# Ragged self-attention on one core: the prologue ahead of the loops is reordered

## The chip, the cores and the metric

The kernel runs on one core of a Trainium2 chip. The core has engines that run beside each other, each with an instruction queue of its own: TensorE (PE in the profile, with PEld for its weight loads), VectorE (DVE), ScalarE (ACT), GpSimd (POOL) and SyncE (SP), which here only issues DMAs and computes addresses. A "q" behind an engine's name (DVEq) means what its queue does itself: register loads, arithmetic on registers, semaphores, branches, issuing of DMAs. The metric is the time of one execution on the device in microseconds (us), a median over runs.

## The reference

32 sequences of up to 512 rows and 512 columns, each with a length drawn between 64 and 511. For each: project to queries, keys and values, then attention with 8 heads of 64 columns over the rows that are alive; rows past the length are zero in the output.

```python
for b in range(batch):
    seq_len = lengths[b]
    qkv = np.matmul(x[b, :seq_len], w_qkv)
    q, k, v = np.split(qkv, 3, axis=-1)          # each to (n_heads, seq_len, head_dim)
    scores = scale * np.matmul(q, k.transpose(0, 2, 1))
    attn = np.exp(scores - np.max(scores, axis=-1, keepdims=True))
    attn = attn / (np.sum(attn, axis=-1, keepdims=True) + 1e-08)
    output[b, :seq_len] = np.matmul(attn, v).transpose(1, 0, 2).reshape(seq_len, dim)
```

## The kernel before

The sequences are sorted by length on the chip, longest first, and worked off in pairs. There are loops for twelve lengths (512, 448, then 384 down to 96 in steps of 32); each handles the pairs whose longer sequence fits, so its trip count depends on the lengths and is read into registers of each engine at run time. A loop's body works on one sequence at a time (a "position", j = 0 or 1): scores `S` on PE, exponentials on ACT, `A` for attention times values; between them PE projects the next sequence: `Q`, `K` (line 228, `project`) and `V` (line 239, `values`). The order in a body is a string in `ORDER`.

The change touches only `before_loops`, the prologue (below: the head), and one line of setup. The head is a list of named operations, each with an engine, the resources it reads and writes, and code; the order of the list is the order on each engine's queue, and `plan_waits` works out from the resources which semaphores are to be waited on. So moving an operation in the list moves it on its own engine's queue only, and the waits follow.

What the head does, in the order of the data:

- Lengths come in (`row`, `col`); DVE ranks them (`key_row`, `least`, `rank`, `hit_i`, `hit_l`), PE spreads the sorted numbers over the partitions (line 446), DVE stores `order` and `slen`. `least` gives the longest sequence's number early, so that SP can fetch its four tiles of 128 rows (`x0.0` to `x0.3`, line 520).
- Weights in float32 come by DMA in halves (`wv`, `wq`, `wk`, line 336) and are cast to float16 in four chunks of 128 rows (`shorten`, line 622) on ACT and POOL. Every Q block needs all four chunks of W_q, every K block all four of W_k.
- Each tile of x0 is masked and cast (`cast_tile`, lines 280 to 285), transposed by four matmuls into a bank (`turn`, line 645) and copied out as `xT` (line 654). V0 to V3 need one tile each; Q0 to Q3 and K0 to K3 need all four. Their results go from a bank to SBUF by a copy (line 677).
- The second sequence, x1, is cast and transposed the same way (banks 3 to 6); the third, x2, is cast by POOL and transposed by DMA.
- From the sorted lengths DVE makes `more`, `counts`, `shifted`, `ends_f` and `ends`: the trip counts, packed in three words. `read_ends` (lines 594 to 616) loads each word into a register of an engine and takes it apart with shifts and masks.
- POOL fills the columns of `et` that a loop's exponentials leave out (14 memsets, line 479), and PE runs 24 matmuls on the identity (line 551) while nothing else is ready.

SP issues, in this order: lengths, W_v, x0's tiles, W_q, W_k, x1, x2. Banks are eight parts of PSUM; an operation that writes a bank waits for the copy that last read it. Before, K0 takes bank 1, which Q2 used.

Of the kernel before, what the change touches and what calls it, by code (L numbers as in the profile page):

```python
# [14 lines left out]
ALU = mybir.AluOpType  # L15
AX = mybir.AxisListType

P = 128
# [130 lines left out]
def kernel(  # L149
# [8 lines left out]
    nc = tc.nc  # L158
    B, MAXS, D = x.shape
# [38 lines left out]

    why = "sorted on the chip from indices 0 to 31, and counts of 0 to 16"

    WARM = 24
    LOOPS = [512, 448, *range(384, 64, -32)]

    ORDER = {
# [56 lines left out]
    def copy_on(act):  # L261
        return nc.scalar.copy if act else nc.vector.tensor_copy
# [33 lines left out]
    def before_loops():  # L296
# [4 lines left out]
        def op(name, eng, emit, reads=(), writes=(), dma=False):  # L301
            ops.append(Op(name, eng, emit, tuple(reads), tuple(writes), dma))

        def small(name, eng, emit, reads=(), shape=(B, B), dtype=FP32):

            t = const.tile(list(shape), dtype, name=f"h_{name}")
            op(name, eng, lambda: emit(t), reads, (name,))
            return t
# [20 lines left out]
            dma=True,  # L329
        )  # L330

        def weights(name, tile_, m0, c0, c1):
            op(
                f"{name}{c0}",
                "SP",
                lambda: sp.dma_start(out=tile_[:, c0:c1, :], in_=w_in[:, c0:c1, m0 : m0 + D]),
                (),
                [f"{name}.{c}" for c in range(c0, c1)],
                dma=True,
            )  # L340
# [5 lines left out]
        def iota(pattern, up, base=0):  # L346
# [35 lines left out]
        def copied(name, eng, source, after, shape=(B, B), dtype=FP32):  # L382
            return small(
                name, eng, lambda t: copy_on(eng == "ACT")(out=t, in_=source), after, shape, dtype
            )

        idx_f = copied("idx_f", "DVE", idx_i, ("idx_i",))
        idc_f = copied("idc_f", "DVE", idc_i, ("idc_i",), (B, 1))
        iota_f = copied("iota_f", "DVE", iota_i, ("iota_i",), (P, NT))
        ident16 = copied("ident16", "DVE", ident, ("ident",), (P, P), F16)  # L390

# [78 lines left out]
                :, :, N // 2 :  # L470
            ]

        for n in range(NT, 0, -1):
            N = min(N for N in LOOPS if tiles(N) == n)
            for e, et in enumerate(e_bufs if n > 1 else e_bufs[0:2]):
                op(
                    f"et{e}.{N}",
                    "POOL",
                    lambda et=et, N=N: pool.memset(left_out(et, N), 0x3C003C00),
                    ("order", f"et{e}"),  # L480
                    (f"et{e}",),
                )

        def mask(b, pos):
            op(
# [63 lines left out]
        def warm():  # L549
            for k in range(WARM):  # L550
                nc.tensor.matmul(banks[3][:, 0:P], ident16, ident16, start=True, stop=True)

        op("warm", "PE", warm, ("ident16",), ("bk3",))

        more = small(
            "more",
            "DVE",
            lambda t: dve.tensor_tensor(
                out=t,
                in0=slen.rearrange("p (j two) -> p j two", two=2)[:, :, 0]  # L560
                .unsqueeze(1)
                .broadcast_to([P, COUNTS, B // 2]),
                in1=limits,
                op=ALU.is_gt,
            ),
            ("slen", "limits"),
            (P, COUNTS, B // 2),
        )
        counts = small(
            "counts",  # L570
            "DVE",
            lambda t: dve.tensor_reduce(out=t, in_=more, axis=AX.X, op=ALU.add),
            ("more",),
            (P, COUNTS),
        )
        shifted = small(
            "shifted",
            "DVE",
            lambda t: dve.tensor_tensor(out=t, in0=counts, in1=shifts, op=ALU.mult),
            ("counts", "shifts"),  # L580
            (P, COUNTS),
        )
        ends_f = small(
            "ends_f",
            "DVE",
            lambda t: dve.tensor_reduce(
                out=t, in_=shifted.rearrange("p (g k) -> p g k", k=4), axis=AX.X, op=ALU.add
            ),
            ("shifted",),
            (P, COUNTS // 4),  # L590
        )
        op("ends", "DVE", lambda: dve.tensor_copy(out=ends_i, in_=ends_f), ("ends_f",), ("ends",))

        def read_ends(e, part=None):
            def load():
                eng = EN[e]
# [61 lines left out]
                (f"xT{b}.{t}",),  # L658
            )

        def step(name, bank, eng):
# [15 lines left out]
            op(name, eng, lambda: copy_on(eng == "ACT")(out=to, in_=of_), (bank,), (made,))  # L677
# [19 lines left out]
        def twos(source):  # L697
# [16 lines left out]
        op(  # L714
            "alive",
            "DVE",
# [19 lines left out]
            (P, B // 2),  # L736
        )
        joined("table", four, computed, 20, ("four", "computed"), table)
        step("V2", "bk4", "DVE")
        shorten("wq", w_q, 0, 2, "ACT")  # L740
        op(
            "M",
            "DVE",
# [35 lines left out]
        step("Q3", "bk6", "ACT")  # L779
        read_ends("PE", 1)  # L780
        read_ends("PE", 2)
# [11 lines left out]
        read_ends("SP")  # L793


        def casts():
# [15 lines left out]
        fetch("LD1", 0, 1, 3, 0, NT)  # L812


        op("joinPE", "PE", lambda: None, [f"xT1.{t}" for t in range(NT)], [f"bk{k}" for k in range(3, 7)])
# [6 lines left out]
    def tiles(N):  # L822
        return -(-N // P)
# [440 lines left out]
    with tc.tile_critical():  # L1264
# [100 lines left out]
```

## Time and profile before

| | |
|---|---|
| runs | 344.72, 345.69, 346.73 us; median 345.69 |
| profiled execution | 345.26 us, span 343.4 us |
| PE busy | 326.6 us, 95% |
| ACT, DVE, POOL busy | 262.7, 215.3, 97.9 us |
| first score matmul of the first loop | 22.73 us |
| DMA | 73.07 MB, mean 213 GB/s |

A timeline row reads: start and length in us, engine and line, operation, what it writes and reads, the shape, the count of merged instructions, and in brackets the idle time before it and what ended that. Line numbers are those of the kernel before. Matmuls overlap in these rows, so the stage's pace is the distance between starts. The trace begins a little after the execution does and ends before it: the profiled execution's 345.26 us hold 1.9 us that lie outside the span.

### The profile page before, as it was taken

To read this page: it belongs to the slowest core of one execution; us is meant where nothing else is said; L and a number is where in the kernel's file an instruction comes from. 1 tells how busy PE (TensorE), PEld (TensorE's weight loads), DVE (VectorE), ACT (ScalarE), POOL (GpSimd) and SP (SyncE) were. 2 spreads that over 40 slices of the span, in tenths; PEclk is the share of its full clock that TensorE was granted. 3 is DMA by queue.
4 is the path that set the end of the run, shared out by engine and by line. 5 is a ranking of instruction groups with operands and counts; after the bars stand their busy time and mean duration, and the time that the engine had idled before them with its cause. 6 is when DMAs were issued, how large, how long until landed. Compare 5 with 4: busy or idle time off the path is not lost.

```text
span 343.4 us, 10664 instructions
## 1 busy us (share of the span) xinstructions
PE 326.6 (95%) x3846; PEld 201.4 (59%) x3846; DVE 215.3 (63%) x657; ACT 262.7 (77%) x410; POOL 97.9 (29%) x124
## 2 busy tenths in 40 slices
PE   4999999999999999999999999999999999999971
PEld 3444545464555555556655656675677776777751
DVE  6556666667667565465555566677775547777664
ACT  4369899797877878889888898777567788678741
POOL 5466040404030330331133033113222342242311
PEclk9999999999999999999999999999999999999996
DMA  6975974483638936957849549869986656669742
GB/s 224 369 239 131 334 170 135 146 282 90 223 67 287 304 83 226 283 177 285 271 139 307 195 152 338 248 241 238 266 244 198 171 168 216 207 171 238 229 142 79
DMA packets 76060, 73.07 MB, mean 213 GB/s; under 512 B 45808, under 2 KB 45808, under 8 KB 76016
## 3 DMA queue, kind: packets, MB, share of 16 engines
q1 hardware_dynamic: 75968, 72.51, 72.4%
q8 instruction: 24, 0.39, 0.5%
q14 instruction: 20, 0.16, 0.2%
q10 hardware_dynamic: 48, 0.00, 0.0%
HBM read 28.32 MB, written 33.55 MB: 180 GB/s over the span
## 4 chain that ended last, share of the span: by engine, by line
PE 89%; DVE 3%; DMA 2%; issue 1%; SPq 1%; ACT 1%; DVEq 1%; POOL 0%; POOLq 0%
PE banks L228 36%; PE banks L239 21%; PE banks L1065 17%; PE banks L981 15%; DMA out_dram<-out_nat 1%; DVE out_nat L1086 1%; DMA x_nat<-in_x_dram 1%; SPq L255 1%; DVE rcp L1078 1%; DVE qz L677 1%; PE banks L645 1%; DVE v_aug L1039 0%; DVEq L600 0%; DVE rcp L1075 0%; DVE v_aug L677 0%
## 5 line engine op out<-in xcount | busy, mean ns | idle before, releaser
L995 ACT ACTIVATE et<-banks 128x704 f16<-128x704 f32 (+6 forms) x264 | 195.9, 813 | 37.6 <-PE banks L981 36.5
L285 POOL TENSOR_TENSOR x<-x_nat,mask 128x512 f16<-128x512 f32 x87 | 88.3, 1039 | 233.6 <-DVE mask L874 218.3
L228 PE MATMUL banks<-xT,w_r 128*128 128x352 f16 (+11 forms) x1024 | 146.5, 288 | 1.5 <-ACT qz L1023 0.6
L228 PEld LDWEIGHTS banks<-xT,w_r 128*128 128x128 f16 x1024 | 85.0, 98 | 41.6 <-issue 8.7
L239 PE MATMUL banks<-w_r,xT 128*128 128x512 f16 x332 | 85.2, 382 | 0.4 <-ACT xT L654 0.2
L1065 PEld LDWEIGHTS banks<-v_aug,et 128*128 128x128 f16 x1792 | 66.2, 98 | 22.6 <-issue 7.7
L1065 PE MATMUL banks<-v_aug,et 128*128 128x65 f16 x1792 | 74.3, 194 | 1.0 <-ACT et L995 0.7
L1086 DVE TENSOR_TENSOR out_nat<-banks,rcp 128x256 f32<-128x256 f32 (+1 forms) x136 | 64.1, 472 | 5.9 <-DMA out_dram<-out_nat 1.3
L981 PE MATMUL banks<-qz,kT 64*128 64x352 f16 (+11 forms) x640 | 61.6, 298 | 2.8 <-DVE out_nat L1086 1.8
L1075 DVE RECIPROCAL rcp<-banks 128x4 f32<-128x4 f32 (+1 forms) x136 | 25.1, 185 | 44.4 <-PE banks L1065 43.2
L1039 DVE CAST v_aug<-banks 128x512 f16<-128x512 f32 x58 | 40.1, 692 | 18.4 <-PE banks L239 18.2
L239 PEld LDWEIGHTS banks<-w_r,xT 128*128 128x128 f16 x332 | 28.3, 98 | 30.9 <-issue 4.6
L981 PEld LDWEIGHTS banks<-qz,kT 64*128 64x128 f16 x640 | 23.1, 94 | 34.0 <-issue 26.0
L1023 DVE CAST qz<-banks 128x352 f16<-128x352 f32 (+4 forms) x39 | 22.8, 586 | 27.4 <-PE banks L228 27.4
L1023 ACT CAST kT<-banks 128x352 f16<-128x352 f32 (+4 forms) x55 | 26.8, 488 | 13.7 <-PE banks L228 12.8
L1078 DVE TENSOR_TENSOR rcp<-rcp,v_aug 128x4 f32<-128x4 f32 (+1 forms) x136 | 26.1, 192 | 4.7
L1023 ACT CAST qz<-banks 128x320 f16<-128x320 f32 (+5 forms) x52 | 24.5, 477 | 4.9 <-PE banks L228 3.6
L1023 DVE CAST kT<-banks 128x320 f16<-128x320 f32 (+4 forms) x36 | 19.9, 556 | 8.2 <-PE banks L228 7.3
L1039 ACT CAST v_aug<-banks 128x512 f16<-128x512 f32 x21 | 12.5, 596 | 6.1 <-PE banks L239 5.8
L874 DVE TENSOR_SCALAR mask<-alive 128x4 f32 x32 | 5.9, 184 | 5.9 <-issue 5.9
L950 DVE TENSOR_SCALAR v_aug<-alive 128x24 f16 (+3 forms) x32 | 7.2, 224 | 0.0
L446 PE MATMUL banks<-h_hit_i,h_ones 32*128 32x32 f16 x1 | 0.2, 203 | 4.7 <-DVE h_hit_i L429 4.7
(68 smaller groups left out, 48.9 us busy)
## 6 DMA issues: line engine op xcount, KB each, us to landing
x_nat<-in_x_dram SPq DMA_DIRECT2D x12, 768.0 KB, 5.6
out_dram<-out_nat SPq DMA_DIRECT2D x12, 768.0 KB, 4.0
x_nat<-in_x_dram SPq DMA_DIRECT2D x14, 512.0 KB, 4.0
x_nat<-in_x_dram SPq DMA_DIRECT2D x7, 1024.0 KB, 6.7
out_dram<-zeros SPq DMA_DIRECT2D x12, 512.0 KB, 5.4
out_dram<-out_nat SPq DMA_DIRECT2D x12, 512.0 KB, 3.0
out_dram<-out_nat SPq DMA_DIRECT2D x4, 1024.0 KB, 4.7
out_dram<-zeros SPq DMA_DIRECT2D x12, 256.0 KB, 5.4
```

What stands on the lines that cost most here:

```text
L228: last = nc.tensor.matmul(dst[:, 0:N], w_r[:, c, w0 : w0 + P], xT[:, c, 0:N], start=(c == 0), stop=(c == NC - 1),)
L239: last = nc.tensor.matmul(pv, xT[:, c, t * P : (t + 1) * P], w_r[:, c, 2 * D : 3 * D], start=(c == 0), stop=(c == NC - 1),)
L285: return engine.tensor_tensor(out=x16, in0=x32, in1=live.broadcast_to([P, D]), op=ALU.mult)
L950: return nc.vector.tensor_scalar(out=v_bufs[o][:, 0:n, :, HD], in0=alive[:, bass.ds(at("DVE") + (j + 1), 1), 0:n] .rearrange("p o t -> p ( ...
L981: last = nc.tensor.matmul(psc[par][:, x * n128 : x * n128 + N], kT[r, i, kt * P : (kt + 1) * P], qz[r, i, 0:N], start=True, stop=True,)
L995: return nc.scalar.activation(out=et[:, :, x0:x1, 0:N], in_=got.rearrange("p j (x q) -> p j x q", q=n128)[:, :, x0:x1, 0:N], func=AF.Exp, ...
L1023: return copy_on(act)(out=buf[:, ms, 0:N], in_=bank[:, 0 : gm * N].rearrange("p (m q) -> p m q", q=N),)
L1039: return copy_on(act)(out=v_bufs[o][:, t, :, 0:HD], in_=bank.rearrange("p (h d) -> p h d", d=HD))
L1065: last = nc.tensor.matmul(pav[:, g, qt, :], e_bufs[e][:, c0 + qt * P : c0 + (qt + 1) * P], v_aug[:, kt, h, :], start=(kt == 0), stop=(kt = ...
L1075: return nc.vector.reciprocal(out=rcp, in_=pav[:, :, :, HD])
L1078: return nc.vector.tensor_tensor(out=rcp, in0=rcp, in1=v_aug[:, 0:n, h0 : h0 + heads, HD].rearrange("p t g -> p g t"), op=ALU.mult,)
L1086: return nc.vector.tensor_tensor(out=o_t[:, 0:n, h0 * HD : (h0 + heads) * HD].rearrange("p t (g d) -> p g t d", d=HD), in0=pav[:, :, :, 0:HD],
```

## The change

All of it lies ahead of the loops:

- W_q is fetched by two DMAs from ACT's queue, behind ACT's cast of W_v's chunk 0; on SP, W_k's follow x0's directly. W_v's chunks 1 and 3 are cast by POOL instead of ACT.
- PE's 24 matmuls on the identity become four groups: 6 on `ones` over 512 columns as soon as that is set, 7 on the identity over 512 columns, and 5 and 6 over 128 columns between the first transposes and V0.
- POOL's 14 fills come in three parts: 4 after `ends`, 5 after W_q's casts, 5 after W_k's.
- `shifted`, `ends_f` and `ends` move on DVE from before x0's first cast to behind its third.
- Each engine reads its three words of loop ends at different places between its other work (DVE, ACT and POOL had read all three at once).
- x0's last tile is cast by DVE instead of POOL; V1 and V2 stand on PE before that tile's transposes, and the copies of V0 and V1 are moved behind other work on DVE.
- K0 to K3 use banks 3, 4, 5 and 7. x1's transposes stand between K1 and K2 (before: between K2 and K3), in the order 0, 1, 3, 2, through banks 0, 1, 2 and 6. x1's casts go to DVE, ACT, POOL, DVE (before: POOL, DVE, POOL, ACT). Q1's copy goes to ACT; K3's to DVE.
- `idc_f` is cast by ACT, followed by 16 increments of an otherwise unused semaphore on its queue; the semaphore increments that set up DVE's counts are made by SP.

```diff
-    WARM = 24
+        def spaced(e, count):
+            def pad():
+                for _ in range(count):
+                    EN[e].sem_inc(passed, 1)
+            op(f"spaced{e}{len(ops)}", e, pad)
...
+        def warm(name, source, count, repeats, after):
+            rows = source.shape[0]
+            wide = source.unsqueeze(1).broadcast_to([rows, repeats, P])
+            out = banks[3][:, 0 : repeats * P].rearrange("p (r q) -> p r q", q=P)
+            def matmuls():
+                for k in range(count):
+                    last = nc.tensor.matmul(out, source, wide, start=True, stop=True)
+                return last
+            op(name, "PE", matmuls, after, ("bk3",))
+        warm("warm0", ones16, 6, 4, ("ones",))
...
-        idc_f = copied("idc_f", "DVE", idc_i, ("idc_i",), (B, 1))
+        idc_f = copied("idc_f", "ACT", idc_i, ("idc_i",), (B, 1))
+        spaced("ACT", 16)
...
-        weights("wq", w_q, 0, 0, NC // 2)
-        weights("wq", w_q, 0, NC // 2, NC)
         weights("wk", w_k, D, 0, NC // 2)
         weights("wk", w_k, D, NC // 2, NC)
...
+        warm("warm1", ident16, 7, 4, ("ident16",))
...
-        for c in range(NC):
-            shorten("wv", w_v, 2 * D, c, "ACT")
+        shorten("wv", w_v, 2 * D, 0, "ACT")
+        shorten("wv", w_v, 2 * D, 1, "POOL")
+        weights("wq", w_q, 0, 0, NC // 2, "ACT")
+        weights("wq", w_q, 0, NC // 2, NC, "ACT")
+        shorten("wv", w_v, 2 * D, 2, "ACT")
+        shorten("wv", w_v, 2 * D, 3, "POOL")
+        (more, counts)
         cast_tile(0, 0, "DVE")
...
         turn(0, 0, "bk4", "DVE")
+        warm("warm2", ident16, 5, 1, ("ident16",))
         turn(0, 1, "bk5", "ACT")
+        warm("warm3", ident16, 6, 1, ("ident16",))
         cast_tile(0, 2, "DVE")
-        cast_tile(0, 3, "POOL")
-        step("V0", "bk0", "DVE")
+        (shifted, ends_f, ends)
+        copy_V0 = step("V0", "bk0", "DVE", True)
         turn(0, 2, "bk6", "DVE")
+        cast_tile(0, 3, "DVE")
+        copy_V0()
+        read_ends("ACT", 0)
+        read_ends("ACT", 1)
+        fill(4, ("ends",))
+        copy_V1 = step("V1", "bk1", "DVE", True)
+        copy_V2 = step("V2", "bk4", "DVE", True)
+        turn(0, 3, "bk3", "DVE")
+        copy_V1()
         shorten("wq", w_q, 0, 0, "ACT")
-        step("V1", "bk1", "DVE")
-        turn(0, 3, "bk3", "ACT")
         shorten("wq", w_q, 0, 1, "POOL")
+        read_ends("POOL", 0)
+        shorten("wq", w_q, 0, 2, "ACT")
+        shorten("wq", w_q, 0, 3, "POOL")
+        read_ends("POOL", 1)
+        fill(5, ())
+        step("V3", "bk5", "ACT")
+        copy_V2()
+        read_ends("ACT", 2)
+        read_ends("DVE", 0)
...
-        read_ends("DVE")
-        step("V3", "bk5", "ACT")
-        read_ends("ACT")
-        shorten("wq", w_q, 0, 3, "POOL")
         shorten("wk", w_k, D, 0, "POOL")
-        shorten("wk", w_k, D, 2, "POOL")
+        shorten("wk", w_k, D, 1, "POOL")
         step("Q0", "bk2", "DVE")
         fetch("x2", 0, 1, 1, 0, NT)
-        shorten("wk", w_k, D, 1, "POOL")
-        step("Q1", "bk0", "DVE")
+        read_ends("DVE", 1)
+        step("Q1", "bk0", "ACT")
         read_ends("PE", 0)
+        shorten("wk", w_k, D, 2, "POOL")
         shorten("wk", w_k, D, 3, "ACT")
+        fill(5, ())
         step("Q2", "bk1", "DVE")
-        read_ends("POOL")
-        cast_tile(1, 0, "POOL")
-        cast_tile(1, 2, "POOL")
+        read_ends("PE", 1)
+        read_ends("POOL", 2)
         step("Q3", "bk6", "ACT")
-        read_ends("PE", 1)
         read_ends("PE", 2)
-        cast_tile(1, 1, "DVE")
-        step("K0", "bk1", "DVE")
-        cast_tile(1, 3, "ACT")
-        step("K1", "bk2", "ACT")
-        step("K2", "bk0", "DVE")
-        for t, (bank, eng) in enumerate(
-            (("bk3", "DVE"), ("bk4", "ACT"), ("bk5", "DVE"), ("bk6", "ACT"))
-        ):
+        cast_tile(1, 0, "DVE")
+        cast_tile(1, 1, "ACT")
+        cast_tile(1, 2, "POOL")
+        cast_tile(1, 3, "DVE")
+        step("K0", "bk3", "DVE")
+        read_ends("DVE", 2)
+        step("K1", "bk4", "ACT")
+        for t, bank, eng in ((0, "bk0", "DVE"), (1, "bk1", "ACT"), (3, "bk2", "ACT"), (2, "bk6", "DVE")):
             turn(1, t, bank, eng)
-        step("K3", "bk7", "ACT")
+        step("K2", "bk5", "DVE")
+        step("K3", "bk7", "DVE")
         read_ends("SP")
...
-                EN[owner[name]].sem_inc(sems[name], unit(name) * amount)
+                (nc.sync if owner[name] == "DVE" else EN[owner[name]]).sem_inc(sems[name], unit(name) * amount)
```

More of the change, by code (lines that the diff above doesn't have):

```diff
@@ L330, in before_loops, with weights @@
         )
-        def weights(name, tile_, m0, c0, c1):
+        def weights(name, tile_, m0, c0, c1, queue="SP"):
             op(
                 f"{name}{c0}",
-                "SP",
-                lambda: sp.dma_start(out=tile_[:, c0:c1, :], in_=w_in[:, c0:c1, m0 : m0 + D]),
+                queue,
+                lambda: EN[queue].dma_start(out=tile_[:, c0:c1, :], in_=w_in[:, c0:c1, m0 : m0 + D]),
                 (),
@@ L471, in left_out, with fill @@
             ]
-        for n in range(NT, 0, -1):
-            N = min(N for N in LOOPS if tiles(N) == n)
-            for e, et in enumerate(e_bufs if n > 1 else e_bufs[0:2]):
+        fills = [
+            (e, et, N)
+            for n in range(NT, 0, -1)
+            for N in [min(N for N in LOOPS if tiles(N) == n)]
+            for e, et in enumerate(e_bufs if n > 1 else e_bufs[0:2])
+        ]
+        def fill(count, after):
+            for e, et, N in fills[:count]:
                 op(
@@ L479, in before_loops @@
                     lambda et=et, N=N: pool.memset(left_out(et, N), 0x3C003C00),
-                    ("order", f"et{e}"),
+                    (*after, f"et{e}"),
                     (f"et{e}",),
                 )
+            del fills[:count]
         def mask(b, pos):
@@ L547, in before_loops @@
         fetch("x1.2", 1, 1, 0, NT // 2, NT)
[L549 to L592, printed above, removed]
+        warm("warm1", ident16, 7, 4, ("ident16",))
         def read_ends(e, part=None):
@@ L659, in turn, with step @@
             )
-        def step(name, bank, eng):
+        def step(name, bank, eng, apart=False):
             kind, k = name[0], int(name[1])
@@ L676, in step @@
             op(name.lower(), "PE", matmuls, reads, (bank,))
-            op(name, eng, lambda: copy_on(eng == "ACT")(out=to, in_=of_), (bank,), (made,))
-        for c in range(NC):
-            shorten("wv", w_v, 2 * D, c, "ACT")
+            copy = lambda: copy_on(eng == "ACT")(out=to, in_=of_)
+            copied = lambda: op(name, eng, copy, (bank,), (made,))
+            return copied if apart else copied()
+        shorten("wv", w_v, 2 * D, 0, "ACT")
[4 more added lines that the diff above has]
+        shorten("wv", w_v, 2 * D, 3, "POOL")
+        more = small(
+            "more",
+            "DVE",
+            lambda t: dve.tensor_tensor(
+                out=t,
+                in0=slen.rearrange("p (j two) -> p j two", two=2)[:, :, 0]
+                .unsqueeze(1)
+                .broadcast_to([P, COUNTS, B // 2]),
+                in1=limits,
+                op=ALU.is_gt,
+            ),
+            ("slen", "limits"),
+            (P, COUNTS, B // 2),
+        )
+        counts = small(
+            "counts",
+            "DVE",
+            lambda t: dve.tensor_reduce(out=t, in_=more, axis=AX.X, op=ALU.add),
+            ("more",),
+            (P, COUNTS),
+        )
         cast_tile(0, 0, "DVE")
@@ L704, in before_loops @@
         turn(0, 0, "bk4", "DVE")
+        warm("warm2", ident16, 5, 1, ("ident16",))
         turn(0, 1, "bk5", "ACT")
+        warm("warm3", ident16, 6, 1, ("ident16",))
         cast_tile(0, 2, "DVE")
-        cast_tile(0, 3, "POOL")
-        step("V0", "bk0", "DVE")
-        turn(0, 2, "bk6", "DVE")
+        shifted = small(
+            "shifted",
+            "DVE",
+            lambda t: dve.tensor_tensor(out=t, in0=counts, in1=shifts, op=ALU.mult),
+            ("counts", "shifts"),
+            (P, COUNTS),
+        )
+        ends_f = small(
+            "ends_f",
+            "DVE",
+            lambda t: dve.tensor_reduce(
+                out=t, in_=shifted.rearrange("p (g k) -> p g k", k=4), axis=AX.X, op=ALU.add
+            ),
+            ("shifted",),
+            (P, COUNTS // 4),
+        )
+        op("ends", "DVE", lambda: dve.tensor_copy(out=ends_i, in_=ends_f), ("ends_f",), ("ends",))
+        copy_V0 = step("V0", "bk0", "DVE", True)
+        turn(0, 2, "bk6", "DVE")
+        cast_tile(0, 3, "DVE")
[7 more added lines that the diff above has]
+        copy_V1()
         shorten("wq", w_q, 0, 0, "ACT")
-        step("V1", "bk1", "DVE")
-        turn(0, 3, "bk3", "ACT")
         shorten("wq", w_q, 0, 1, "POOL")
+        read_ends("POOL", 0)
[7 more added lines that the diff above has]
+        read_ends("DVE", 0)
         op(
@@ L738, in before_loops @@
         joined("table", four, computed, 20, ("four", "computed"), table)
-        step("V2", "bk4", "DVE")
-        shorten("wq", w_q, 0, 2, "ACT")
         op(
@@ L762, in before_loops @@
         )
-        read_ends("DVE")
-        step("V3", "bk5", "ACT")
-        read_ends("ACT")
-        shorten("wq", w_q, 0, 3, "POOL")
         shorten("wk", w_k, D, 0, "POOL")
-        shorten("wk", w_k, D, 2, "POOL")
+        shorten("wk", w_k, D, 1, "POOL")
         step("Q0", "bk2", "DVE")
         fetch("x2", 0, 1, 1, 0, NT)
-        shorten("wk", w_k, D, 1, "POOL")
-        step("Q1", "bk0", "DVE")
+        read_ends("DVE", 1)
+        step("Q1", "bk0", "ACT")
         read_ends("PE", 0)
+        shorten("wk", w_k, D, 2, "POOL")
         shorten("wk", w_k, D, 3, "ACT")
+        fill(5, ())
         step("Q2", "bk1", "DVE")
-        read_ends("POOL")
-        cast_tile(1, 0, "POOL")
-        cast_tile(1, 2, "POOL")
-        step("Q3", "bk6", "ACT")
-        read_ends("PE", 1)
-        read_ends("PE", 2)
-        cast_tile(1, 1, "DVE")
-        step("K0", "bk1", "DVE")
-        cast_tile(1, 3, "ACT")
-        step("K1", "bk2", "ACT")
-        step("K2", "bk0", "DVE")
-        for t, (bank, eng) in enumerate(
-            (("bk3", "DVE"), ("bk4", "ACT"), ("bk5", "DVE"), ("bk6", "ACT"))
-        ):
+        read_ends("PE", 1)
+        read_ends("POOL", 2)
+        step("Q3", "bk6", "ACT")
+        read_ends("PE", 2)
+        cast_tile(1, 0, "DVE")
+        cast_tile(1, 1, "ACT")
+        cast_tile(1, 2, "POOL")
+        cast_tile(1, 3, "DVE")
[3 more added lines that the diff above has]
+        for t, bank, eng in ((0, "bk0", "DVE"), (1, "bk1", "ACT"), (3, "bk2", "ACT"), (2, "bk6", "DVE")):
             turn(1, t, bank, eng)
-        step("K3", "bk7", "ACT")
+        step("K2", "bk5", "DVE")
+        step("K3", "bk7", "DVE")
         read_ends("SP")
+        assert not fills
         def casts():
@@ L812, in before_loops @@
         fetch("LD1", 0, 1, 3, 0, NT)
-        op("joinPE", "PE", lambda: None, [f"xT1.{t}" for t in range(NT)], [f"bk{k}" for k in range(3, 7)])
+        op("joinPE", "PE", lambda: None, [f"xT1.{t}" for t in range(NT)], [f"bk{k}" for k in (0, 1, 2, 6)])
         op("joinACT", "ACT", lambda: None, [f"et{e}" for e in range(4)])
```

## The prediction

> **What bounds the kernel now.** I read the page first (busy shares, then the chain that ended last), then the head, which is all that the change touches: the timeline of each engine from 0 to 24 us, the chain of the same stretch, the register loads by line, and the DMA rate by microsecond.
>
> ```profile
> span 343.4 us, 10664 instructions
> ...
> PE 326.6 (95%) x3846; PEld 201.4 (59%) x3846; DVE 215.3 (63%) x657; ACT 262.7 (77%) x410; POOL 97.9 (29%) x124
> ...
> PE 89%; DVE 3%; DMA 2%; issue 1%; SPq 1%; ACT 1%; DVEq 1%; POOL 0%; POOLq 0%
> ```
>
> TensorE (PE) is the bound: 95% busy, 89% of the chain. From the first score matmul of the first loop at 22.73 us the slices read 9 nearly to the end, so whatever brings that matmul forward comes off the end one for one. The question is where the head's 22.73 us go. PE's timeline there (start, length, what; x is the count):
>
> ```profile
> 8.97 1.74 PE L239 MATMUL banks<-w_r,xT 128*128 128x512 f16 x4
> ...
> 10.78 1.03 PE L239 MATMUL banks<-w_r,xT 128*128 128x512 f16 x4
> ...
> 14.03 3.61 PE L228 MATMUL banks<-xT,w_r 128*128 128x512 f16 x16
> 18.12 2.76 PE L228 MATMUL banks<-xT,w_r 128*128 128x512 f16 x12 [0.47 <-DVE qz L677]
> 20.72 1.06 PE L645 MATMUL banks<-h_ident,x 128*128 128x128 f16 x16
> 21.61 1.03 PE L228 MATMUL banks<-xT,w_r 128*128 128x512 f16 x4
> 22.73 1.07 PE L981 MATMUL banks<-qz,kT 64*128 64x512 f16 x6
> ```
>
> The reader sees four stages: values (V), 16 query matmuls at 14.03, three key blocks at 18.12, x1's transposes, the last key block. A run of x16 starts its matmuls 0.216 us apart (3.61 less the last one's 0.38, over 15), so the query stage has issued its last at 14.03 + 16 x 0.216 = 17.48 and could hand over there; keys begin at 18.12. These 0.64 us are the one hole in PE after 14.03. What opens it, from the chain:
>
> ```profile
> 13.07 0.42 DVEq L600
> ...
> 13.94 0.32 DVEq L600
> ...
> 15.24 0.30 DVEq L600
> ...
> 16.18 1.90 DVE qz L677 x3
> 18.07 0.05 issue
> 18.12 2.76 PE banks L228 x12
> ```
>
> VectorE's (DVE's) queue reads three words of loop ends, with shifts and masks between, until 16.13; only then come the three Q copies behind it, and K0 wants bank 1, which the third empties at 18.07. The other ends that matter:
>
> ```profile
> 11.96 0.62 ACT L622 CAST w_r<-w_q 128x512 f16<-128x512 f32 x1 [2.16 <-DMA w_q<-in_w_qkv_dram]
> ...
> 13.30 0.61 POOL L622 CAST w_r<-w_q 128x512 f16<-128x512 f32 x1 [0.70 <-DMA w_q<-in_w_qkv_dram]
> ...
> 16.05 1.17 POOL L622 CAST w_r<-w_k 128x512 f16<-128x512 f32 x2 [0.71 <-DMA w_k<-in_w_qkv_dram]
> ...
> 18.53 0.72 ACT L284 ACTIVATE x<-x_nat,mask 128x512 f16<-128x512 f32 x1 [0.27 <-DMA x_nat<-in_x_dram]
> ...
> 9.33 0.49 DVE L280 TENSOR_SCALAR x<-x_nat,mask 128x512 f16<-128x512 f32 x1 [0.47 <-DMA x_nat<-in_x_dram]
> ```
>
> W_q's second half lands at 13.3 and its last cast ends at 13.91: Q0 at 14.03 waits for that, not for the cold V0. W_k is cast at 17.22, x1's second half lands at 18.5, x0's third tile at 9.33. The DMA engines (last two columns: busy share, GB/s) are full but for 8 to 10 us:
>
> ```profile
> 8.00:9.00 1.00, 0.82 (x9) 0.56 (x8) 0.53 (x2) 0.52 (x1) 0.80 (x5) 1.00 0.69 205
> 9.00:10.00 1.00, 1.00 (x5) 0.43 (x4) 0.49 (x1) 0.58 (x1) 0.00 (x0) 1.00 0.91 281
> 11.00:16.00 5.00, 4.77 (x26) 2.05 (x25) 2.97 (x9) 2.31 (x4) 2.30 (x4) 1.00 1.04 391
> ```
>
> **The change part by part.** *Loop ends on DVE, and banks for keys.* The three words are read after V2's, Q0's and K0's copies. K0 follows its matmuls' start by 1.07 us before (19.19 after 18.12), so Q0's copy starts at about 15.10, not 16.18, and Q2's (DVE) at 16.8; a word costs about 1.1 us of the queue (three took 12.95 to 16.13) and fits between. The third word holds DVE's queue to about 19.9, so T10 comes at 19.9 instead of 19.6; T10 (0.42) and T12 (0.33) end by 21, and the joint that needs them stands behind the last key matmul: nothing. Keys go to banks 3, 4, 5 and 7, whose last readers are V's copies and transposes ended by 14.8, so K0 waits for no copy: K0 at 17.48, **-0.64 us**. Next late is W_k's cast at 17.22, 0.26 before.
>
> *Fills behind casts (POOL).* The 14 fills (3.57 us, 0.26 each) move from 5.2-8.8, where POOL was free, into 4 behind `ends`, 5 behind W_q, 5 behind W_k. With W_q's last cast at 13.91, word 1 (0.8 us from 13.3) and 5 fills end at 15.4; W_k's three casts (0.61, then 0.56 apart) at 17.2; five fills at 18.5, word 2 by about 18.75. K0 keeps 0.2 us of cover; if POOL is 0.5 us later, K0 is 0.3 later. x1's third tile is then cast 18.75 to 19.8 (1.04).
>
> *x1 amid keys.* K0 and K1 run 17.48 to 19.21. Tiles 0, 1 and 3 need casts by 19.2, 19.4, 19.7: DVE 0.48 behind Q2's copy at 17.5, ACT 0.72 behind Q3's copy (18.3 to 19.0), DVE 0.48 from 18.55. Tile 2 goes last, ready at 19.8 when its turn is 19.88. K2 and K3 end at 20.10 + 1.73 = 21.83, the first score 0.26 later as before (22.73 against 21.61 + 0.86): 22.09. The transposes cost what they did; their four copies are covered by K2 and K3. K3's copy goes from ACT (0.585) to DVE (0.69); the third score wants its bank 7 (23.41, just after that copy's 23.26): between 0 and +0.1, I take **+0.10**, as its neighbour ends on that copy. ACT, free of it, can start its first exponential up to 0.5 us earlier; PE then has other work to 26.4, so I take 0.
>
> *Values.* V0 alone ran cold: 0.427 us apart, 1.71 against 0.86. With matmuls of `ones` from about 1.95 (6 x 0.427 = 2.56, ending 4.5, ahead of the spread at 4.74) and of the identity behind, the 5.8 us that warming took (4.74 to 10.55, where the rows turn fast) would be over at 7.8, and x0's last cast is 0.49 on DVE instead of 1.04 on POOL. V3 ends at 13.1 to 13.6, not 13.99. Worth 0 while Q0 waits for W_q; up to 0.9 were W_q earlier. Seven cold identity matmuls (3.0) would hold the first transpose to 8.1 from 7.79: hidden by the same wait. [...]
>
> *W_q by ACT's queue.* Its two issues go out at about 5.3 and 5.8 behind ACT's first cast (5.25), not at 6.47; W_k and x1 follow on SP 0.94 earlier. From 10 us on the DMA engines are full, so this alters who lands first, not the sum. New is that x0's tiles 1 to 3 no longer precede W_q. That matters by one chain: x0's tile 2 is cast (0.49), then `shifted` to `ends` (6.52 to 7.18: 0.66), then ACT reads two words (loads at 14.2 to 15.8 for two: 1.6) ahead of its two W_q casts (1.14), with 0.1 to 0.2 of handing over: Q0 not before tile 2's landing + 4.07. At 9.33 that is 13.40, below the 14.03 of W_q. No row shows two large queues at once. Lower bound: tile 2 as now, or W_q up to 0.7 us earlier because 8 to 10 us fill up. Upper: from 7.2 on tiles 1 and 2 take double, 9.33 + 2.1 = 11.4. At the full 391 GB/s with equal turns, 2 x 0.52 MB take 2.7 us: 9.9, and Q0 at 13.97. I take that, nearest to the full windows: **0**. [...]
>
> *The rest.* DVE's six increments go to SP: 6 x 0.065 = 0.4 us behind SP's at 2.6, done at 3.4 before `least` at 3.65; uncovered it would be 0.1 to 0.4 on x0's issue. ACT's cast of idc and 16 increments (0.2 + 1.0) follow its table load, over by 4.2 before W_v lands at 5.25. W_v's casts shared with POOL: 0.6 sooner, not awaited. x2 still lands behind x1 at 21.9; its transposes land at 31.3 and are first wanted at 42.9. Ends on PE's queue run ahead under matmuls, as before.
>
> **Sum**: -0.64 + 0.10 + 0 = -0.54 against the profiled execution's 345.26: 344.7. That execution is 0.43 under the median shown, 345.69.
>
> **The rivals.** *The front comes forward too* (speaks for it: the thin 8 to 10 us, the cold V0; against: Q0's wait on W_q). W_q lands at 12.6, all POOL work moves by 0.6, Q0 at 13.6, last key at 21.3, first score 21.6: -1.13 + 0.1, 344.2; if V3's 13.1 is all that holds it, 343.7. *Turns between queues make it slower*: x0's tile 2 at 11.0 to 11.4 puts Q0 at 15.07 to 15.47 by the chain above: +1.1 to +1.5 on the sum, 345.8 to 346.2, slower than before. It decides from a landing of 10.5 on (9.96 + 0.54). For: both streams are issued within half a microsecond; against: thin windows that could take W_q for nothing. *The hole only moves*: POOL, which now holds fills and reads among its casts, ends W_k 0.9 late, K0 stays at 18.1, or x1's tile 2 comes at 20.5: 345.3, no change. For: cover of 0.2 us; against: nothing else that is new stands on POOL.
>
> **How the numbers follow.** The forecast 0.42, front forward 0.23, turns 0.22, hole moves 0.13. A half per cent is 1.7 us, about what a measurement of this kernel tells from no change. Faster by more needs more than the whole of the front case: most of its tail and the spread of the runs (344.72 to 346.73), 0.20. Slower by more needs tile 2 beyond 12: 0.12. Range: from 343.4 (front case, 0.3 of spread) to 346.2 (turns).
>
> **What would show it.** After: K0's matmuls right behind Q's with no DVE wait; `qz` on DVE without the 2.10 idle; the first L981 at about 22.1; V0 at 0.86 rather than 1.71; Q0 still near 14.0 behind a W_q cast. Wrong if x0's tile 2 is cast after 10.5, if PE waits for POOL's `w_r` or x1 ahead of keys, or if the first score moves and the end doesn't.

## The result and the profile after

The changed kernel takes 347.55 us (median of 22 runs, 346.14 to 350.73) against 345.49 us of the kernel before (22 runs, 344.43 to 347.69): a ratio of 1.0059, 95% interval 1.0038 to 1.0081. It is 2.06 us slower, where 344.7 was forecast and the range ended at 346.2. The profiled execution took 347.09 us against 345.26: +1.83, and its span is longer by as much:

```profile
span 345.2 us, 10681 instructions
...
PE 329.4 (95%) x3846; PEld 201.3 (58%) x3846; DVE 219.1 (63%) x659; ACT 261.0 (76%) x408; POOL 97.0 (28%) x124
```

PE is still the bound and its share has not moved. Of the 1.83 us, 1.61 are lost in the head. PE's timeline of the kernel after, in the columns of the one before (L238 values, L227 queries and keys):

```profile
15.30 1.04 PE L238 MATMUL banks<-w_r,xT 128*128 128x512 f16 x4 [0.52 <-DVE xT L638]
16.17 5.34 PE L227 MATMUL banks<-xT,w_r 128*128 128x512 f16 x24
...
22.25 1.89 PE L227 MATMUL banks<-xT,w_r 128*128 128x512 f16 x8
...
25.34 1.04 PE L238 MATMUL banks<-w_r,xT 128*128 128x512 f16 x4
```

Three readings. Queries and the first two key blocks are one unbroken row of 24: the hole ahead of K0 is gone. But that row begins at 16.17, not at 14.03. And what stands ahead of it is V3, which waited for the copy of x0's last tile (`xT`), not a cast of W_q. VectorE casts the last two tiles late:

```profile
11.89 0.49 DVE L279 TENSOR_SCALAR x<-x_nat,mask 128x512 f16<-128x512 f32 x1 [2.92 <-DMA x_nat<-in_x_dram]
13.38 0.63 DVE L279 TENSOR_SCALAR x<-x_nat,mask 128x512 f16<-128x512 f32 x1
```

x0's third tile is cast at 11.89 (before: 9.33), the fourth at 13.38 (before: 10.43), each as soon as it has landed (11.87 and 13.36). The chain that ended last runs through the third tile's transfer (before: through the second's, 5.04 to 7.78). A start in it is the moment at which the piece before it let go:

```profile
5.40 6.47 DMA x_nat<-in_x_dram
...
12.43 0.40 PE banks L629 x4
12.83 1.73 PE banks L238 x8
14.56 0.24 PE banks L629 x4
...
14.82 0.43 DVE xT L638
```

So the third tile decides. PE waits 1.23 us for its cast, then does its transposes, V1, V2 and the last tile's transposes in the order of its queue, and V3 follows their copy. The last tile itself was cast by 14.01, before PE got to it at 14.39.

Step by step, in the starts of the rows: Q0 +2.14 (14.03 to 16.17); from Q0 to the end of the last key row 7.97 instead of 8.61, -0.64; from there to the first loop's first values 1.20 (25.34 less 24.14) instead of 1.09, +0.11. The sum is +1.61, and 25.34 stands against 23.73. Matmul by matmul the two traces keep that distance (+1.59) to 119 us; it then grows in steps to +2.08 at 312 us and falls back to +1.83 by the last one.

### The profile page after: what moved, and what is told of

Read it like the earlier page. It is cut to its first block, busy times and chain, and to the rows that moved or that the text cites. A ratio compares the mean times of both kernels' runs of the same rounds, so it can differ in the third digit from the quotient of the medians.

```text
span 345.2 us, 10681 instructions
## 1 busy us (share of the span) xinstructions
PE 329.4 (95%) x3846; PEld 201.3 (58%) x3846; DVE 219.1 (63%) x659; ACT 261.0 (76%) x408; POOL 97.0 (28%) x124
## 4 chain that ended last, share of the span: by engine, by line
PE 89%; DMA 3%; DVE 3%; issue 1%; SPq 1%; ACT 0%; POOL 0%; POOLq 0%; DVEq 0%
PE banks L227 36%; PE banks L238 21%; PE banks L1107 17%; PE banks L1023 15%; DMA x_nat<-in_x_dram 2%; DMA out_dram<-out_nat 1%; DVE out_nat L1128 1%; SPq L254 1%; DVE rcp L1120 1%; PE banks L629 0%; DVE v_aug L1081 0%; SPq L550 0%; DVE rcp L1117 0%; DVE kT L661 0%; ACT qz L1065 0%
## 5 line engine op out<-in xcount | busy, mean ns | idle before, releaser
L284 POOL TENSOR_TENSOR x<-x_nat,mask 128x512 f16<-128x512 f32 x85 | 86.3, 1041 | 232.7 <-DVE mask L916 231.5
L227 PE MATMUL banks<-xT,w_r 128*128 128x352 f16 (+11 forms) x1024 | 146.3, 287 | 1.1 <-ACT qz L1065 0.6
L227 PEld LDWEIGHTS banks<-xT,w_r 128*128 128x128 f16 x1024 | 85.2, 98 | 40.9 <-issue 8.8
L238 PE MATMUL banks<-w_r,xT 128*128 128x512 f16 x332 | 84.3, 380 | 0.7 <-DVE xT L638 0.5
L1081 DVE CAST v_aug<-banks 128x512 f16<-128x512 f32 x58 | 40.1, 692 | 16.7 <-PE banks L238 16.5
L238 PEld LDWEIGHTS banks<-w_r,xT 128*128 128x128 f16 x332 | 28.2, 97 | 30.8 <-issue 4.0
L1065 ACT CAST kT<-banks 128x352 f16<-128x352 f32 (+4 forms) x55 | 26.8, 488 | 13.6 <-PE banks L227 12.8
L916 DVE TENSOR_SCALAR mask<-alive 128x4 f32 x32 | 7.2, 224 | 6.0 <-issue 6.0
L992 DVE TENSOR_SCALAR v_aug<-alive 128x24 f16 (+3 forms) x32 | 8.4, 264 | 0.0
L279 DVE TENSOR_SCALAR x<-x_nat,mask 128x512 f16<-128x512 f32 x5 | 3.3, 669 | 3.5 <-DMA x_nat<-in_x_dram 3.4
```

Source lines behind the costliest of these rows:

```text
L227: last = nc.tensor.matmul(dst[:, 0:N], w_r[:, c, w0 : w0 + P], xT[:, c, 0:N], start=(c == 0), stop=(c == NC - 1),)
L238: last = nc.tensor.matmul(pv, xT[:, c, t * P : (t + 1) * P], w_r[:, c, 2 * D : 3 * D], start=(c == 0), stop=(c == NC - 1),)
L284: return engine.tensor_tensor(out=x16, in0=x32, in1=live.broadcast_to([P, D]), op=ALU.mult)
L992: return nc.vector.tensor_scalar(out=v_bufs[o][:, 0:n, :, HD], in0=alive[:, bass.ds(at("DVE") + (j + 1), 1), 0:n] .rearrange("p o t -> p ( ...
L1065: return copy_on(act)(out=buf[:, ms, 0:N], in_=bank[:, 0 : gm * N].rearrange("p (m q) -> p m q", q=N),)
L1081: return copy_on(act)(out=v_bufs[o][:, t, :, 0:HD], in_=bank.rearrange("p (h d) -> p h d", d=HD))
```

## The experiments

Each ratio is to runs of the kernel before from the same set: their median was 346.28 us (29 runs) for W_q back on SP, W_q alone on ACT's queue, half of W_q and the loop-end reads, and 345.48 us (29 runs) for the others. So ratios can be compared between the sets, and medians cannot.

**W_q back on SP's queue.** One part of the change undone.

```diff
-        weights("wq", w_q, 0, 0, NC // 2, "ACT")
-        weights("wq", w_q, 0, NC // 2, NC, "ACT")
+        weights("wq", w_q, 0, 0, NC // 2)
+        weights("wq", w_q, 0, NC // 2, NC)
         weights("wk", w_k, D, 0, NC // 2)
```

> The changed kernel with W_q's two DMAs back on SP's queue between x0 and W_k; all else of the change stays. Theory (turns between two DMA queues hold x0's tiles back): x0's third tile is cast at about 9.3 instead of 11.9, its last at about 10.6 instead of 13.4, Q0 starts near 14.0 instead of 16.2, the first score near 22.1 instead of 24.1; 0.3 to 0.8 us under the kernel before, some 2.3 under the changed one. Rival (the fills and loop-end reads among POOL's and ACT's casts, or x1 amid the keys, cost the time): the first score stays near 24, the time 1 to 2 us over the kernel before.

Measured: 345.70 us (12 runs), ratio to before 0.9986 [0.9960, 1.0012]; profiled 345.15. VectorE's cast of the third tile, then PE:

```profile
9.19 0.48 DVE L279 TENSOR_SCALAR x<-x_nat,mask 128x512 f16<-128x512 f32 x1
```

```profile
13.11 1.04 PE L238 MATMUL banks<-w_r,xT 128*128 128x512 f16 x4 [0.52 <-DVE xT L640]
13.98 5.34 PE L227 MATMUL banks<-xT,w_r 128*128 128x512 f16 x24
```

The tile is back at 9.19 and Q0 at 13.98, 2.19 earlier than after; the profiled time falls by 1.94 and the ratio from 1.0059 to 0.9986. The loss lies in that one part. It is not ACT's work of issuing: ACT's next cast of W_v starts at 6.46 here and at 6.45 in the kernel after. The rest of the change brings its first loop's values to 23.14, 0.59 ahead of before. V3 gates Q0 here too (W_q's casts end at 13.52), so W_q is no longer the last thing awaited even when x0 is on time.

**W_q on ACT's queue, alone.** The kernel before with only its two W_q fetches moved, behind ACT's cast of W_v's first chunk.

```diff
-        weights("wq", w_q, 0, 0, NC // 2)
-        weights("wq", w_q, 0, NC // 2, NC)
...
+        shorten("wv", w_v, 2 * D, 0, "ACT")
+        weights("wq", w_q, 0, 0, NC // 2, "ACT")
+        weights("wq", w_q, 0, NC // 2, NC, "ACT")
+        for c in range(1, NC):
+            shorten("wv", w_v, 2 * D, c, "ACT")
```

> The kernel before with one part of the change alone: W_q's two DMAs are issued from ACT's queue behind its cast of W_v's chunk 0. Theory (turns): x0's third tile lands at 11.5 to 12, its last at 13 to 13.5 and is cast by POOL until 14.5, Q0 at 16 to 16.5, the first score near 25; 1.5 to 2.5 us slower than the kernel before. Rival (the queue is harmless): within 0.5 us of the kernel before.

Measured: 349.54 us (6 runs), ratio 1.0095 [1.0062, 1.0129]; profiled 348.52. PE of this kernel (L239 values, L228 queries and keys):

```profile
12.91 1.91 PE L239 MATMUL banks<-w_r,xT 128*128 128x512 f16 x4
...
17.15 3.62 PE L228 MATMUL banks<-xT,w_r 128*128 128x512 f16 x16
21.68 2.76 PE L228 MATMUL banks<-xT,w_r 128*128 128x512 f16 x12 [0.91 <-DVE qz L675]
```

x0's third tile is cast at 11.97, as in the kernel after, and Q0 comes 3.12 later than before, beyond the 16 to 16.5 expected. It costs more here than within the change, for two reasons the rows show. V1's four matmuls at 12.91 take 1.91 instead of 1.03, and V2 begins slow too (V2 and V3 are a row of eight in 2.27, where eight take 1.89 in the kernel after). The kernel after has the same wait of 1.23 ahead of the third tile's transposes, and with its new warming does V1 and V2 in a row of eight in 1.89. And the hole ahead of K0 is still there, 0.91 instead of 0.47. So the other parts of the change repaired part of what this one cost.

**Half of W_q on each queue.** The kernel after with W_q's second half moved to SP, ahead of W_k's.

```diff
         weights("wq", w_q, 0, 0, NC // 2, "ACT")
-        weights("wq", w_q, 0, NC // 2, NC, "ACT")
...
+        weights("wq", w_q, 0, NC // 2, NC)
         weights("wk", w_k, D, 0, NC // 2)
```

> The changed kernel with W_q's first half on ACT's queue and its second half on SP's ahead of W_k: half the dose. Theory (turns): x0's second tile still lands late (about 8.8), the third at 11 to 11.5, the last at 12 to 12.5, Q0 at 15.2 to 15.7; about 0.6 to 1.0 us under the changed kernel and 0.8 to 1.3 over the kernel before. Rival (a second queue costs by being there, whatever it carries): the same time as the changed kernel.

Measured: 346.89 us (12 runs), ratio 1.0016 [0.9985, 1.0048], which includes no change; profiled 347.19, no less than the 347.09 of the kernel after. VectorE:

```profile
11.21 0.49 DVE L279 TENSOR_SCALAR x<-x_nat,mask 128x512 f16<-128x512 f32 x1 [2.24 <-DMA x_nat<-in_x_dram]
```

Half the bytes still put the third tile at 11.21 (9.19 with none, 11.89 with all) and Q0 at 15.49; the second tile, expected late, was cast in time (7.83). Q0 is 0.68 earlier than in the kernel after, so in the head the amount counts and not only the second queue, by one profile each. The times do not resolve it. That half of W_q landed at 12.15, x0's last tile at 12.33: the two ran beside each other nearly as long as x0 needed.

**W_q on ACT's queue, but late.** The kernel after with the two fetches moved behind ACT's cast of x0's second tile, so that W_q's transfers begin when x0's are nearly through.

```diff
-        weights("wq", w_q, 0, 0, NC // 2, "ACT")
-        weights("wq", w_q, 0, NC // 2, NC, "ACT")
...
         cast_tile(0, 1, "ACT")
+        weights("wq", w_q, 0, 0, NC // 2, "ACT")
+        weights("wq", w_q, 0, NC // 2, NC, "ACT")
```

> The changed kernel with W_q still on ACT's queue, but issued behind ACT's cast of x0's second tile (at about 7.8 instead of 5.1), so that its bytes start when x0's are nearly through; W_k on SP is issued at 6.3 as in the changed kernel. Theory (two queues take turns, and whatever is wanted first loses): x0's third tile lands at 9.2 to 9.8 and its last at 10 to 11, but W_q now shares with W_k and lands only at 15 to 16, so Q0 starts at 15.8 to 16.5 and the first score at 23.7 to 24.4: no better than the changed kernel. Rival (only x0's delay costs): Q0 near 14, the first score near 22, as with W_q on SP.

Measured: 352.51 us (4 runs), ratio 1.0184 [1.0133, 1.0235]; profiled 354.0. PE, and then the shares of the two queues between 14 and 16 us (q1 is SP's, q10 ACT's; packets, MB, share of the engines' time):

```profile
20.21 7.97 PE L227 MATMUL banks<-xT,w_r 128*128 128x512 f16 x24 [6.22 <-POOL w_r L606]
```

```profile
q10 hardware_dynamic: 213, 0.41, 52.6%
q1 hardware_dynamic: 213, 0.41, 52.4%
```

x0 is untouched (V3 at 12.96), but W_q now shares the DMA engines with W_k and x1, in these two microseconds evenly, and its last chunks are cast only from 19.45. The direction was as expected, the size was not: W_q's halves landed at 16.76 and 19.43 instead of 15 to 16, and Q0 came at 20.21. PE waits 6.22 us. It then pays a second time: these 24 matmuls take 7.97 us instead of 5.34. The windows give PE's busy time first and, third from the end, the clock that TensorE was granted:

```profile
11.93:15.34 3.41, 1.54 (x10) 0.52 (x8) 2.49 (x9) 0.00 (x0) 0.00 (x0) 1.00 1.02 351
15.34:18.75 3.41, 0.00 (x0) 0.00 (x0) 0.00 (x0) 0.62 (x1) 0.61 (x1) 0.50 1.05 407
```

The clock halves at 15.34 and is back only at 25.6. With W_q too early it is x0 that is late, with W_q late it is W_q; in SP's single queue (W_q back on SP) x0's third tile was cast at 9.19, W_q's last casts ended at 13.52 and Q0 came at 13.98.

**The loop-end reads alone.** The kernel before with VectorE's three words read at three places instead of one.

```diff
-        read_ends("DVE")
+        read_ends("DVE", 0)
...
         step("Q0", "bk2", "DVE")
+        read_ends("DVE", 1)
...
         step("K0", "bk1", "DVE")
+        read_ends("DVE", 2)
```

> The kernel before with one part alone: DVE reads its three words of loop ends behind V2's, Q0's and K0's copies instead of all three behind V2's. By the prediction's sum the hole of 0.64 us ahead of K0 closes to 0.1 (Q2's copy ends at 17.5 and empties bank 1): 0.4 to 0.6 us faster. Rival (the hole only moves, W_k's casts or x1's then hold PE): within 0.2 us of the kernel before.

Measured: 346.29 us (12 runs), ratio 1.0003 [0.9976, 1.0029]; profiled 345.37. Its PE (L228 queries and keys, L239 values), first the head and then 310 to 312 us:

```profile
13.81 6.50 PE L228 MATMUL banks<-xT,w_r 128*128 128x512 f16 x28
...
310.67 1.03 PE L239 MATMUL banks<-w_r,xT 128*128 128x512 f16 x4
312.10 0.71 PE L228 MATMUL banks<-xT,w_r 128*128 128x160 f16 x8 [0.40 <-issue]
```

The same stretch of the kernel before:

```profile
311.16 1.03 PE L239 MATMUL banks<-w_r,xT 128*128 128x512 f16 x4
312.10 0.71 PE L228 MATMUL banks<-xT,w_r 128*128 128x160 f16 x8
```

Queries and three key blocks are one row of 28, but not one without a wait: 28 matmuls 0.216 apart would take 6.21, and the row takes 6.50. K0 starts at 17.54, 0.28 late, right behind Q2's copy (the two Q copies on DVE run from 16.20 to 17.49), for it still wants Q2's bank 1. So the reads alone take 0.36 of the 0.64 us, where 0.54 were expected. Ahead of that Q0 is 0.22 earlier than before; W_q landed 0.23 earlier in this execution (13.01 against 13.24), which is not the edit's doing. Behind it x1's transposes lose 0.14. First values of the loop: 23.29 against 23.73, -0.44, of which the edit made about half.

That lead lasts 287 us, and then both kernels start the same projection at 312.10. Ahead of it PE's queue waits, by their semaphore, for the DMA transposes of the next x: from 311.23 before, from 310.74 here, and to 312.04 in both. SP began to issue them at 306.94 before and at 306.44 here, so they took 5.07 us until they had landed, and here 5.56. In the ten profiles of this document they take 4.67 to 5.61, and why they vary was not tested. So this lead was lost to a longer transfer in one execution, not to a fixed end: with K3's copy back on ACT (below) they take 4.67, and that kernel gains 0.08 on the kernel before at this place.

With W_q on SP the same projection starts at 311.96, and of its lead of 0.59 only 0.12 is left at the last matmul. Part of this was lost earlier, in the loops. The kernel after and five others derived from it (all but the one with W_q late, which was not compared) lose 0.14 to 0.19 us between 123 and 130 us, 0.05 to 0.06 at 287 and 0.10 to 0.11 at 301 (times of the kernel before), some 0.3 in all, whichever queue W_q is on. The two derived from the kernel before do not lose this. At 287 PE is idle for 0.80 instead of 0.69: behind the wait that ends last there, its queue goes through three more waits of 0.11 each instead of two, and at 301 through two instead of one. So waits inside the loops changed as well, though the edit lies ahead of them; how they did was not followed up, and what is lost near 125 is open.

A lead of 0.1 to 0.6 us is 0.03 to 0.17% of the time, and the intervals of these versions reach 0.2 to 0.3% to either side. No version of the head that is faster at 23 us is measurably faster at the end.

**The old warming, without W_q's move.** W_q on SP, and PE's 24 matmuls on the identity instead of the four groups.

```diff
-        warm("warm0", ones16, 6, 4, ("ones",))
-        warm("warm1", ident16, 7, 4, ("ident16",))
+        warm("warm1", ident16, 24, 1, ("ident16",))
...
-        warm("warm2", ident16, 5, 1, ("ident16",))
-        warm("warm3", ident16, 6, 1, ("ident16",))
```

> W_q back on SP, and of the rest of the change the four groups of warming matmuls replaced by the 24 of the kernel before. The prediction held that warming earlier is worth nothing while Q0 waits for W_q. If so: V0 runs cold (about 1.7 us for four), Q0 still at 14.0 to 14.1, time as with W_q on SP. Rival (with W_q earlier, V3 is what Q0 waits for, so the cold V0 is paid): Q0 at 14.5 to 14.9, 0.5 to 0.9 us slower than with W_q on SP.

Measured: 345.80 us (10 runs), ratio 1.0006 [0.9978, 1.0033]; profiled 345.65. V0 on PE:

```profile
9.02 1.90 PE L238 MATMUL banks<-w_r,xT 128*128 128x512 f16 x4
```

V0 takes 1.90 instead of 1.03, and Q0 comes at 14.48 against 13.98 and, in the next kernel, 14.30. So the new warming is worth 0.2 to 0.5 us at Q0 once V3 gates it. The times do not resolve that.

**K3's copy back on ACT.** W_q on SP and:

```diff
-        step("K3", "bk7", "DVE")
+        step("K3", "bk7", "ACT")
```

> W_q back on SP, and K3's copy on ACT as in the kernel before. By the prediction's term of +0.10 the third score, which waits for bank 7, comes 0.10 us sooner after the last key matmul (1.04 to 0.93). Rival: the wait there has another end and nothing moves. Too small for the times; read in the trace.

Measured: 346.07 us (10 runs), ratio 1.0016 [0.9984, 1.0048]; profiled 345.11. From the first score to the first values is 1.16 (22.20 to 23.36) instead of 1.26 (21.88 to 23.14 with the copy on VectorE): 0.10 of the head, below what the times can tell.

**x0's last tile transposed ahead of V2.** The kernel just above, with the last tile's transposes moved ahead of V2's matmuls on PE, so that its copy has V2's time as cover.

```diff
+        turn(0, 3, "bk3", "DVE")
         copy_V2 = step("V2", "bk4", "DVE", True)
-        turn(0, 3, "bk3", "DVE")
```

> W_q back on SP, K3's copy on ACT, and the transposes of x0's last tile ahead of V2 on PE instead of behind it. With W_q on SP, V3 waits 0.5 us for that tile's copy and Q0 waits for V3 (13.98), while W_q's casts end at 13.5. If so: Q0 at 13.5 to 13.6, the first score at 21.4 to 21.5, 0.4 to 0.6 us under W_q on SP and about 1 us under the kernel before. Rival (PE then waits for the cast of that tile ahead of V2 and loses the same): no change against W_q on SP.

Measured: 345.21 us (12 runs), ratio 0.9986 [0.9964, 1.0008]; profiled 347.12. From V0's start to Q0's is 4.60 us (10.04 to 14.64) against 4.59 in both kernels with the old order (9.39 to 13.98, 9.71 to 14.30). The wait of 0.52 ahead of V3 is gone, but PE now waits 0.36 ahead of the transposes for the tile's cast, and V0, which began slow here, takes 0.17 more. The rival held, with PE's own order behind it: the tile had landed at 10.23, but DVE casts it only at 11.83, behind its copy of the third tile, and that copy waited for the third tile's transposes, which stand behind V0 on PE. The profiled execution is 1.9 us above the median, and the windows of its tail show a reason of its own (same columns):

```profile
331.20:334.60 3.40, 1.64 (x35) 1.32 (x34) 1.91 (x7) 1.05 (x3) 0.00 (x0) 1.00 0.30 96
334.60:338.00 3.40, 3.31 (x31) 1.90 (x28) 1.89 (x9) 0.94 (x3) 1.04 (x1) 0.50 0.20 71
```

Its clock was halved for one stretch of 3.4 us. The kernel after, in the same two windows, has a clock of 1.00. None of the versions with W_q on SP is told apart from the kernel before by its time; all of their ratios are below the kernel after's 1.0059, though one interval (to 1.0048, with K3's copy on ACT) overlaps with its own, which begins at 1.0038.

## Why the prediction was wrong

**W_q by ACT's queue: wrong, and this decides.** The step took x0's third tile at 9.9 "at the full 391 GB/s with equal turns", hence Q0 at 13.97 and a cost of 0; it measured +2.14 at Q0. The equal turns were the author's assumption. Neither half held. The queues between 7 and 11 us, in the kernel after:

```profile
q10 hardware_dynamic: 379, 0.75, 55.7%
q1 hardware_dynamic: 239, 0.43, 29.3%
```

and before:

```profile
q1 hardware_dynamic: 634, 1.18, 93.5%
```

Both kernels move 1.18 MB in these four microseconds, 295 GB/s. The thin windows did not take W_q for nothing; the second queue added no byte. (With W_q back on SP the same four microseconds moved 1.28 MB.) And of those bytes ACT's queue had 0.75 and SP's 0.43, not half each. By the measured share, x0's second and third tiles (0.52 MB) are through between 11 us (0.43 MB) and 12 us (0.61 MB), and the tile was cast at 11.89: beyond the 11.4 that stood as the upper bound, because that bound doubled the old times and so allowed SP half of the bytes, and SP had 0.43 of 1.18 MB. W_q gained little and lost more: its halves landed at 11.63 and 14.49, before at 11.94 and 13.24. The prediction had named a cast of this tile after 10.5 as a sign of being wrong.

The rival, and the upper bound with it, had the direction right. How two queues share is not shown: the late-W_q run has equal shares for two microseconds, 213 packets each, in the kernel after they were 379 to 239, and no run says why. With the same 1.18 MB in both kernels, the transfer that was first in line lost its place: x0's third tile was cast at 11.89 instead of 9.33.

**The chain that was followed was not the longest.** The working followed the third tile to ACT's casts of W_q: landing + 4.07, which gives 15.94 from 11.87; the last of these casts in fact ended at 15.65. Q0 came at 16.17, landing + 4.30, by PE's own order: the third tile's transposes (12.43), V1 and V2, the last tile's transposes (14.39), its copy (14.82) and V3 (15.30). The working gave V3 an end of 13.1 to 13.6 and called it hidden by the wait for W_q; with the third tile late it became the wait. The rival of turns between queues had the cause (x0's tiles held back by W_q's transfer) and the decisive point (a landing beyond 10.5), and was short by 0.7 to 1.1 us at Q0: +2.14, where its own landings give +1.0 to +1.4 (its text has +1.1 to +1.5).

**The hole: right.** -0.64 forecast, -0.64 between Q0 and the last key row. The loop-end reads alone give 0.36 of it; the 0.28 left there is the wait for bank 1, and with the keys on other banks none is left. POOL's cover held: no wait for `w_r` stands ahead of K0, and x1 amid the keys cost nothing.

**K3's copy: right.** +0.10 forecast; +0.11 against before, and 0.10 by the run that moves it back.

**Warming: a condition that lapsed.** "Worth 0 while Q0 waits for W_q" was right as worded, but in none of the runs derived from the changed kernel with W_q early enough does Q0 wait for W_q: V3 is last. There it is worth 0.2 to 0.5, and it shielded the kernel after from the slow V1 (1.91 for four) and V2 that the old warming shows under the same delay. It was to be over at 7.8; in the kernel after the rows turn fast at about 9.7 (four transposes take 0.63 from 7.88 and 0.42 from 9.59).

**One for one to the end: not shown.** A delay of 1.61 at the first loop came out as 1.83, and leads of 0.44 and 0.59 came out as a loss of 0.11 and a lead of 0.12. The prediction took the loops for the same in both kernels. In the traces the changed one loses some 0.3 us in them, and the DMA wait near 312 us, against the kernel before, adds up to 0.5 or takes 0.1 off from one profile to the next. Without W_q's move the prediction would still have said 344.7, and that profiled execution took 345.15. The chance of a loss over 0.5% was given as 0.12, from a landing beyond 12 alone; with the path that in fact was longest, 11.9 was enough. One smaller reading was off and carried no weight: the last of the four DMA transposes issued from 26 us on lands at 32.46, not at 31.3.

## What to carry to other kernels

Here a transfer moved to a second queue did not fill gaps: it took its share from what was already under way (0.75 of the 1.18 MB that one queue had moved from 7 to 11 us). So ask who is now late, and follow every piece of the delayed transfer to its consumer, along the order of each engine's queue too, not only the one with the longest known chain. One queue in order of need was itself a schedule here: Q0 at 13.98, against 16.17 with two. And a lead won in a head has to be followed to the last instruction: here what was lost at waits further down (some 0.3 us) and the spread of one transfer's length (4.67 to 5.61 us) were about as large as the leads (0.44 and 0.59).

## What the runs showed of the hardware

- Two queues' shares in packets differed by run and moment. In the kernel after, ACT's queue had 379 to SP's 239 from 7 to 11 us. In the late-W_q run it had 141 to 177 from 12 to 14 us, 213 to 213 from 14 to 16, and 165 to 259 from 16 to 18. What sets the share is open.
- In the late-W_q run the fetches were issued from 7.67 us, but ACT's queue moved nothing until 10 us and 0.03 MB between 10 and 12, while SP's moved 0.68; the cause is open.
- TensorE's granted clock went from 1.00 to 0.50 behind stretches in which PE had been busy for 1.54 of 3.41 us (the late-W_q run, up to 15.34), 1.64 of 3.40 (x0's last tile ahead of V2, up to 334.60) and 1.80 of 3.41 (the kernel before, up to 338.10), so work in such a stretch did not prevent it. The stretches were laid so as to end where the clock changed. Their busy time alone does not settle it: the same execution of the kernel before has 1.74 in the 3.41 us from 329.79 to 333.20, and its clock reads 1.00 up to 338.10. Once at 0.50, in the late-W_q run, it stayed there through 1.95 busy of 3.41 us (18.75 to 22.16) and 3.42 of 3.42 (22.16 to 25.58), and read 1.00 from about there on. What sets it is not shown.
- The profile's granted clock reads 1.00 in the windows from 4 to 16 us of the kernel with W_q alone on ACT's queue, while V1's four matmuls there take 1.91 us (12.91 to 14.82) instead of 1.03. In this head the pace has to be read from the rows, not from that column.
